# Output weights split on ScalarE and VectorE, router steps of a tile set between the matmuls of the next, ranking in two parts

## The chip, the core and the metric

The kernel runs as one program on one core of one Trainium2 chip. The metric is device time in microseconds (us) from launch to the end of the program. A core has five engines that work side by side and wait for each other through semaphores: TensorE (PE; its weight loads are listed as PEld), VectorE (DVE), ScalarE (ACT), GpSimd (POOL) and SyncE (SP), which here only issues transfers. Transfers run on 16 DMA engines of the core.

## The reference, cut to what matters

Two layers of a hybrid encoder over 528 tokens (16 learned ones, called meta, and 512 real ones) of 1024 channels. In each layer three head groups (RWKV-7, differential attention, gated linear attention) give 1024 mixed channels, an output projection adds them to the residual, and 16 experts each take their best 66 tokens:

```python
mix = jnp.concatenate([y_a, y_b, y_c], axis=-1).astype(h.dtype)
h = h + jnp.einsum("blc,cd->bld", mix, w_out[l])
h = h + expert_choice_ffn(rms_norm(h, norm2_g[l]), router[l], e_w1[l], e_w3[l], e_w2[l])

def expert_choice_ffn(u, router, w1, w3, w2):
    cap = EC_FACTOR * L // N_EXPERTS                    # 66
    aff = jax.nn.softmax(jnp.einsum("bld,de->ble", u, router).astype(jnp.float32), axis=-1)
    gates, idx = lax.top_k(jnp.swapaxes(aff, 1, 2), cap)
    xs = jax.vmap(lambda ub, ib: ub[ib])(u, idx)
    hid = jax.nn.silu(jnp.einsum("becd,edf->becf", xs, w1)) * jnp.einsum("becd,edf->becf", xs, w3)
    ys = jnp.einsum("becf,efd->becd", hid, w2) * gates[..., None].astype(u.dtype)
```

## The kernel before

Products run as three matmuls on operands that are split into a high part and a low rest: a weight `w` becomes `wh` (a copy in a shorter format) and `wl = w - wh`.

One layer goes through these stages. The input projection and the three head groups come first; the attention sweeps its 528 queries in the tiles 1, 2, 0, 3, 4 of `TOK` (tile 0 holds the 16 meta tokens, the others 128 tokens each). Its softmax is a chain of short VectorE and ScalarE steps around matmuls. While it runs, GpSimd splits the eight blocks of the output weights, `wo_h` by a copy (L966) and `wo_l` by a subtraction (L967), from two buffers `wo`.

The projection loop then takes the tiles 1, 2, 3, 4, 0. For a tile it makes two halves `c` of 512 output channels with 24 matmuls each (L1026), adds them to the residual `h` (L1029), and does the router's part: transposes `ut` (L1033) and their copies `hT`, the sum of squares (L1044) and a chain of some ten VectorE steps for the reciprocal root (L183 to L191), the logits `plg` (L1049), a softmax over 16 experts (L1052 to L1056), the transpose `pt` of it (L1058) into the table `aff` of 16 experts by tokens, and the normalised row `u`, scaled on ScalarE (L1060) and multiplied by the gain on GpSimd (L1061), which is written to `ubuf` in memory (L1062).

The ranking `top` takes the eight largest values of each expert's row at a time (L1007), finds their places (L1010) and strikes them out (L1009), nine times over 512 tokens; the 16 meta tokens are ranked apart and merged. The indices `idx` (L1078) then drive the gather of an expert's rows (L1118), an indirect transfer issued by GpSimd.

The expert stage streams 192 weight tiles of 1408 KB through nine buffers, five of which can be filled during the projection. Each half of a tile is split by ScalarE (`wh`, L1111) and VectorE (`wl`, L1112) into four buffers each, and feeds TensorE (`up_tile` and `down`, L1156 and L1217). The first four subtractions are ordered behind `idx`.

The code is written in program order, and a scheduler lays each engine's instructions out in a fixed queue of its own; within a queue they run in order. `behind(inst, mark)` keeps two instructions in that order without a wait.

Of the kernel before, what the change touches and what calls it, by code (L numbers as in the profile page):

```python
# [23 lines left out]
D = 1024  # L24
# [81 lines left out]
def body(ctx: ExitStack, tc: tile.TileContext, a, out, dbg=None, depth=DEPTH, stop=None):  # L106
# [61 lines left out]
    def behind(inst, mark):  # L168
        if mark is not None:
            tc.add_manual_dep(inst.ins, mark.ins.name,  # L170
                              mybir.DependencyInfo(mybir.DependencyClass.NoSync, mybir.DependencyReason.DATA),
                              reason="issue order")
        return inst
# [37 lines left out]
    for l in range(depth):  # L211
# [751 lines left out]
        for k in range(KT):  # L963
            w = op.tile([128, D], F32, name="wo", bufs=2)
            nc.sync.dma_start(w, a["w_out"][l, k])
            G.tensor_copy(wo_h[:, k], w)  # L966
            G.tensor_sub(wo_l[:, k], w, wo_h[:, k].bitcast(F32))  # L967
        if "a" in order:
            bank_pool("s")
            attention(ap_, *hd)  # L970
            bank_pool("mm")
        parts.close()
# [21 lines left out]
        with tc.tile_pool(name="rt", bufs=1, side="right", reuse_waits="tile") as rtp:  # L994
            g2b = rtp.tile([128, D], F32, name="g2b")
            nc.sync.dma_start(g2b, a["norm2_g"][l:l + 1].to_broadcast([128, D]))
            aff = rtp.tile([NE, SEQ], F32, name="aff")
            affm = rtp.tile([NE, NM], F32, name="affm")

            def top(x, n, name):  # L1000
                v = rtp.tile([NE, n], F32, name=f"top_v{name}")
                iu = rtp.tile([NE, n], U32, name=f"top_u{name}")
                fi = rtp.tile([NE, n], F32, name=f"top_i{name}")
# [14 lines left out]
            for t in (1, 2, 3, 4, 0):  # L1018
                o, R = TOK[t]
                p = mm_tile("po")  # L1020
                h = load_h(op, h_src, t, 3)[:R]
                for c in range(2):
                    n = 0
                    for ww, mm in ((wo_h, mh), (wo_h, ml), (wo_l, mh)):
                        for k in range(KT):
                            T.matmul(p[:R, c, :], mm[:, k, o:o + R], ww[:, k, c * 512:(c + 1) * 512],  # L1026
                                     start=(n == 0), stop=(n == 23))
                            n += 1
                    V.tensor_add(two(h)[:, c], p[:R, c], two(h)[:, c])  # L1029
                nc.sync.dma_start(hbuf[o:o + R, :], h)  # L1030
                pt = [rw_tile(q, "ut") for q in range(2)]
                for k in range(KT):
                    T.transpose(pt[k // 4][:, (k % 4) * 128:(k % 4) * 128 + R], h[:, k * 128:(k + 1) * 128],  # L1033
                                ident[:R, :R])
                hT = rtp.tile([128, 2, 4, 128], F32, name="hT", bufs=2)
                for q in range(2):
# [3 lines left out]
                    else:  # L1040
                        V.tensor_copy(hT[:, q, :, :R], src)
                u = rtp.tile([128, D], F32, name="u2", bufs=2)
# [5 lines left out]
                for k in range(KT):  # L1048
                    T.matmul(p[:R, :NE], hT[:, k // 4, k % 4, :R], rt[:, k, :], start=(k == 0), stop=(k == KT - 1))  # L1049
# [6 lines left out]
                V.tensor_scalar(lg[:R], lg[:R], mx[:R, 3:4], None, op0=OP.mult)  # L1056
                pt = sm_tile("pt")
                T.transpose(pt[:NE, :R], lg[:R], ident[:R, :R])  # L1058
                V.tensor_copy(aff[:, o - NM:o - NM + R] if t else affm, pt[:NE, :R])
                A.activation(u[:R], h, AF.Identity, scale=rs)  # L1060
                G.tensor_mul(u[:R], u[:R], g2b[:R])  # L1061
                G.dma_start(ubuf[o:o + R, :], u[:R])  # L1062
            vm, im = top(affm, NM, "m")
            va, ia = top(aff, 72, "a")
            V.tensor_scalar(ia, ia, float(NM), None, op0=OP.add)
            at_ = slice(CAP - NM, CAP)
            rev = lambda x: x[:, ::-1]
            take = rtp.tile([NE, NM], F32, name="take")
            V.tensor_tensor(take, rev(vm), va[:, at_], op=OP.is_ge)
            V.tensor_tensor(va[:, at_], va[:, at_], rev(vm), op=OP.max)  # L1070
            V.tensor_sub(im, im, rev(ia[:, at_]))
            V.tensor_mul(im, im, rev(take))
            V.tensor_add(ia[:, at_], ia[:, at_], rev(im))
# [17 lines left out]
        with tc.tile_pool(name="mw", bufs=1, reuse_waits="tile") as mw, \  # L1091
                tc.tile_pool(name="mh", bufs=1, reuse_waits="tile") as mhl, \
                tc.tile_pool(name="moe", bufs=2, reuse_waits="tile") as mo:
            ring, gathers, splits = [0], [], []
# [253 lines left out]
```

## Time and profile before

| what | us |
|---|---|
| three timed runs, median (lowest to highest) | 2734.44 (2730.94 to 2737.09) |
| the profiled execution: its own time | 2737.51 |
| the profiled execution: its span | 2735.7 |
| busy in the span: TensorE, VectorE, ScalarE, GpSimd | 2518.9, 2170.6, 1604.4, 441.3 |

The span runs from the first to the last instruction; the 1.8 us beside it lie around the program. Busy times overlap, so that they don't add up. The mean granted clock of TensorE was 0.947 of full speed. All times of the trace below are counted from the start of the span. The first layer takes about the first half of it, the second the rest.

### The profile page before, as it was taken

Reading aid. Unit: us, or ns where it says so; the run is one execution under the profiler, and the core shown is the slowest. Engines: PE = TensorE matmul, PEld = TensorE weight load, DVE = VectorE, ACT = ScalarE, POOL = GpSimd, SP = SyncE. Lnnn points to the kernel's source line nnn. Section 1 sums busy time; section 2 is a strip of 40 time slices with the busy share of each in tenths; the row PEclk is TensorE's granted clock in tenths of the full one; section 3 lists DMA queues with packets and bytes.
Section 4 is the critical chain, followed back from the end, with each engine's and each line's share of the span. In section 5 each row is a group of like instructions: output and inputs, shape, how many; then the busy total and the mean of one; then the engine's idle time right before and its main releaser. Section 6 shows DMA issues by size and latency. Waiting matters only on the chain.

```text
span 2735.7 us, 46610 instructions
## 1 busy us (share of the span) xinstructions
PE 2518.9 (92%) x18586; PEld 1981.8 (72%) x18586; DVE 2170.6 (79%) x3293; ACT 1604.4 (59%) x2107; POOL 441.3 (16%) x545
## 2 busy tenths in 40 slices
PE   7899999786999999999788899998689999999995
PEld 6778786565777777778587787755467787877783
DVE  3557667758999999999735676687589999999995
ACT  3324334425888888788542343344268888888884
POOL 3113322213000000000121133241120000000000
PEclk9878999997999999999997789999889999999998
DMA  3101101148999999999420111022499999999993
GB/s 129 47 24 60 37 25 51 64 172 312 408 400 405 403 399 409 397 412 404 174 77 32 40 44 49 13 73 93 148 358 393 413 397 411 399 409 401 407 402 117
DMA packets 84682, 643.30 MB, mean 235 GB/s; under 512 B 12592, under 2 KB 13040, under 8 KB 35312
## 3 DMA queue, kind: packets, MB, share of 16 engines
q1 hardware_dynamic: 75936, 618.16, 57.0%
q0 software_dynamic: 8528, 22.15, 3.3%
q8 instruction: 146, 2.39, 0.4%
q14 instruction: 72, 0.59, 0.1%
HBM read 617.05 MB, written 19.40 MB: 233 GB/s over the span
## 4 chain that ended last, share of the span: by engine, by line
PE 41%; DVE 5%; issue 2%; ACT 2%; DMA 1%; POOL 0%; DVEq 0%; SPq 0%; ACTq 0%; POOLq 0%
PE py L1217 9%; PE pj L288 5%; PE h1a L1156 4%; PE h3a L1156 3%; PE h1b L1156 3%; PE h3b L1156 3%; PE h1T L1156 1%; PE h3T L1156 1%; PE po L1026 1%; PE po L730 1%; DMA hbuf<-yo,idx 1%; PE S L898 1%; PE pl L473 1%; PE up L307 1%; PE py L563 0%
## 5 line engine op out<-in xcount | busy, mean ns | idle before, releaser
L1112 DVE TENSOR_TENSOR wl<-w,wh 128x1408 fp32r<-128x1408 f32 (+2 forms) x768 | 1212.7, 1617 | 59.9 <-ACT wh L1111 35.3
L1111 ACT ACTIVATE wh<-w 128x1408 fp32r<-128x1408 f32 (+2 forms) x768 | 1042.7, 1378 | 196.9 <-PE py L1217 78.5
L1217 PE MATMUL py<-wh,hh 128*66 128x512 f32 (+1 forms) x768 | 289.2, 377 | 4.3 <-ACT hh L1197 4.3
L1217 PE MATMUL py<-wh,hl 128*66 128x512 f32 (+1 forms) x768 | 288.7, 376 | 0.8 <-DVE hl L1198 0.8
L1217 PE MATMUL py<-wl,hh 128*66 128x512 f32 (+1 forms) x768 | 288.4, 375 | 0.0
L1222 POOL DMA_INDIRECT hbuf<-yo,idx x32 | 54.9, 1714 | 1190.0 <-ACT yo L1221 1076.6
L1156 PE MATMUL h1a<-wh,xx 128*66 128x512 f32 x512 | 186.1, 414 | 1.1 <-DVE xx L1134 1.1
L1156 PE MATMUL h3a<-wh,xx 128*66 128x512 f32 x512 | 182.8, 408 | 0.0
L1156 PE MATMUL h1b<-wh,xx 128*66 128x512 f32 x512 | 176.3, 410 | 0.0
L1156 PE MATMUL h3b<-wh,xx 128*66 128x512 f32 x512 | 174.7, 407 | 0.0
L1156 PE MATMUL h1T<-xx,wh 128*128 128x132 f32 x768 | 172.1, 224 | 0.0
L1156 PE MATMUL h3T<-xx,wh 128*128 128x132 f32 x768 | 171.3, 223 | 0.0
L288 PE MATMUL pj<-uh,wh 128*128 128x264 f32 (+1 forms) x896 | 166.5, 314 | 5.2 <-ACT kS L344 5.0
L288 PE MATMUL pj<-ul,wh 128*128 128x264 f32 (+1 forms) x896 | 162.2, 313 | 0.0
L288 PE MATMUL pj<-uh,wl 128*128 128x264 f32 (+1 forms) x896 | 155.6, 303 | 0.0
L1217 PEld LDWEIGHTS py<-wh,hh 128*66 128x66 f32 x768 | 105.2, 137 | 64.1 <-ACT hh L1197 4.5
L1217 PEld LDWEIGHTS py<-wl,hh 128*66 128x66 f32 x768 | 105.1, 137 | 60.6 <-issue 1.0
L1156 PE MATMUL h1T<-xx,wl 128*128 128x66 f32 x768 | 148.9, 194 | 0.0
L1156 PEld LDWEIGHTS h3T<-xx,wh 128*128 128x128 f32 x768 | 146.6, 191 | 2.7
L1156 PEld LDWEIGHTS h1T<-xx,wh 128*128 128x128 f32 x768 | 148.3, 193 | 0.0
L1156 PE MATMUL h3T<-xx,wl 128*128 128x66 f32 x768 | 148.3, 193 | 0.0
L1217 PEld LDWEIGHTS py<-wh,hl 128*66 128x66 f32 x768 | 105.3, 137 | 59.1 <-DVE hl L1198 1.5
(444 smaller groups left out, 5061.9 us busy)
## 6 DMA issues: line engine op xcount, KB each, us to landing
w<-in_e_w SPq DMA_DIRECT2D x384, 1408.0 KB, 10.9
w<-in_w_in SPq DMA_DIRECT2D x56, 512.0 KB, 3.5
wo<-in_w_out SPq DMA_DIRECT2D x16, 512.0 KB, 3.5
h<-hbuf SPq DMA_DIRECT2D x12, 512.0 KB, 4.7
swp<-raw SPq DMA_DIRECT2D x64, 66.0 KB, 2.0
h<-in_x SPq DMA_DIRECT2D x8, 512.0 KB, 7.2
hbuf<-h SPq DMA_DIRECT2D x8, 512.0 KB, 2.8
ubuf<-u POOLq DMA_DIRECT2D x8, 512.0 KB, 4.6
```

Source lines behind the costliest of these rows:

```text
L288: T.matmul(p[:M, c, :HL], ww[:, k, :M], uu[:, k, c * HL:(c + 1) * HL], start=(n == 0), stop=(n == 23))
L307: T.matmul(p[:, c, :HL], lhsT, rhs[:, c * HL:(c + 1) * HL], start=True, stop=True)
L473: T.matmul(pl[:, b, :], flat(BC[m][:, jm[m]]), az[:, m].rearrange("p x q n -> p (x q n)"), start=True, stop=True)
L730: T.matmul(o_, qd[d][hc(h), j * CH:(j + 1) * CH], kv[hc(h), d, j, :], start=False, stop=(d == 1), tile_position=(32 * h, 64 * (h % 2)))
L898: behind(T.matmul(p[:R], qk[0, h][:, qo:qo + R], qk[1, h][:, c, NM:], start=True, stop=True), mark)
L1026: T.matmul(p[:R, c, :], mm[:, k, o:o + R], ww[:, k, c * 512:(c + 1) * 512], start=(n == 0), stop=(n == 23))
L1111: A.activation(wh, w[:, lo:hi], AF.Copy)
L1112: splits.append(behind(V.tensor_sub(wl, w[:, lo:hi], wh.bitcast(F32)), chosen if len(splits) < 4 else None))
L1156: T.matmul(o_, l_, r_, start=s0, stop=s1)
L1217: T.matmul(py[:CAP, c, d0:d0 + n], x[:, kk, :], ww[:, at0 - lo:at0 - lo + n], start=(kk == 0 and i_ == 0), stop=(kk == FK - 1 and i_ == 2))
L1222: G.indirect_dma_start(out=hbuf[:, :], out_offset=bass.IndirectOffsetOnAxis(ap=idx[:CAP, e:e + 1], axis=0), in_=yo[:CAP], in_offset=None, ...
```

## The change

Four things are edited.

The output weights are no longer split by GpSimd. Four of the eight blocks are loaded ahead of the attention, and the code that splits them, copies on ScalarE and subtractions on VectorE, is written behind it.

The projection goes through the tiles 1, 2, 0, 3, 4 and runs block by block of the weights. The router's part of a tile is cut into `turn`, `affinity` and `ranked`, which are set at fixed places between the matmuls of the next tile: behind its first half, behind 12 matmuls of its second half, and behind that half. The product for `u` is one VectorE instruction.

The ranking is done in two parts: the 272 tokens of tiles 0, 1 and 2 as soon as those are through, the 256 of tiles 3 and 4 at the end, and the two lists of 66 are merged by a comparison of one with the reverse of the other.

The first four subtractions of the expert stage wait, by a semaphore, for the first gather.

```diff
+
+    def after(inst, mark):
+        tc.add_manual_dep(inst.ins, mark.ins.name,
+                          mybir.DependencyInfo(mybir.DependencyClass.Sync, mybir.DependencyReason.DATA),
+                          reason="the port is the gather's first")
...
         wo_h = op.tile([128, KT, D], F32R, name="wo_h")
         wo_l = op.tile([128, KT, D], F32R, name="wo_l")
-        for k in range(KT):
-            w = op.tile([128, D], F32, name="wo", bufs=2)
-            nc.sync.dma_start(w, a["w_out"][l, k])
-            G.tensor_copy(wo_h[:, k], w)
-            G.tensor_sub(wo_l[:, k], w, wo_h[:, k].bitcast(F32))
+        wos = ExitStack()
+        wsp = wos.enter_context(tc.tile_pool(name="wos", bufs=1, side="left", reuse_waits="tile"))
+        wo_r = []
+
+        def wo_load():
+            w = wsp.tile([128, D], F32, name="wo", bufs=4)
+            nc.sync.dma_start(w, a["w_out"][l, len(wo_r)])
+            wo_r.append(w)
+
+        for k in range(4):
+            wo_load()
         if "a" in order:
             bank_pool("s")
             attention(ap_, *hd)
             bank_pool("mm")
+        for k in range(KT):
+            A.activation(wo_h[:, k], wo_r[k], AF.Copy)
+            V.tensor_sub(wo_l[:, k], wo_r[k], wo_h[:, k].bitcast(F32))
+            if len(wo_r) < KT:
+                wo_load()
+        wos.close()
...
-            aff = rtp.tile([NE, SEQ], F32, name="aff")
-            affm = rtp.tile([NE, NM], F32, name="affm")
+            early = TOK[3][0]
+            aff = rtp.tile([NE, L], F32, name="aff")
...
-                fi = rtp.tile([NE, n], F32, name=f"top_i{name}")
+                fi = iu.bitcast(F32)
...
-            for t in (1, 2, 3, 4, 0):
+            def turn(t, h):
                 o, R = TOK[t]
-                p = mm_tile("po")
-                h = load_h(op, h_src, t, 3)[:R]
-                for c in range(2):
-                    n = 0
-                    for ww, mm in ((wo_h, mh), (wo_h, ml), (wo_l, mh)):
-                        for k in range(KT):
-                            T.matmul(p[:R, c, :], mm[:, k, o:o + R], ww[:, k, c * 512:(c + 1) * 512],
-                                     start=(n == 0), stop=(n == 23))
-                            n += 1
-                    V.tensor_add(two(h)[:, c], p[:R, c], two(h)[:, c])
                 nc.sync.dma_start(hbuf[o:o + R, :], h)
                 pt = [rw_tile(q, "ut") for q in range(2)]
                 for k in range(KT):
-                    T.transpose(pt[k // 4][:, (k % 4) * 128:(k % 4) * 128 + R], h[:, k * 128:(k + 1) * 128],
-                                ident[:R, :R])
+                    mark = T.transpose(pt[k // 4][:, (k % 4) * 128:(k % 4) * 128 + R], h[:, k * 128:(k + 1) * 128],
+                                       ident[:R, :R])
...
+                return hT, mark
+
+            def affinity(t, h, p, hT):
+                o, R = TOK[t]
...
+                    mark = T.matmul(p[:R, :NE], hT[:, k // 4, k % 4, :R], rt[:, k, :], start=(k == 0),
+                                    stop=(k == KT - 1))
...
+                return lg, u, rs, mark
+
+            def ranked(t, h, lg, u, rs):
+                o, R = TOK[t]
                 pt = sm_tile("pt")
                 T.transpose(pt[:NE, :R], lg[:R], ident[:R, :R])
-                V.tensor_copy(aff[:, o - NM:o - NM + R] if t else affm, pt[:NE, :R])
-                A.activation(u[:R], h, AF.Identity, scale=rs)
-                G.tensor_mul(u[:R], u[:R], g2b[:R])
+                V.tensor_copy(aff[:, o:o + R], pt[:NE, :R])
+                V.scalar_tensor_tensor(u[:R], h, rs, g2b[:R], op0=OP.mult, op1=OP.mult)
                 G.dma_start(ubuf[o:o + R, :], u[:R])
-            vm, im = top(affm, NM, "m")
-            va, ia = top(aff, 72, "a")
-            V.tensor_scalar(ia, ia, float(NM), None, op0=OP.add)
-            at_ = slice(CAP - NM, CAP)
-            rev = lambda x: x[:, ::-1]
-            take = rtp.tile([NE, NM], F32, name="take")
-            V.tensor_tensor(take, rev(vm), va[:, at_], op=OP.is_ge)
-            V.tensor_tensor(va[:, at_], va[:, at_], rev(vm), op=OP.max)
-            V.tensor_sub(im, im, rev(ia[:, at_]))
-            V.tensor_mul(im, im, rev(take))
-            V.tensor_add(ia[:, at_], ia[:, at_], rev(im))
+
+            tops, last = {}, None
+            for t in (1, 2, 0, 3, 4):
+                o, R = TOK[t]
+                p = mm_tile("po")
...
+
+                def project(terms, mark=None):
+                    for k, i, c in terms:
+                        ww, mm = ((wo_h, mh), (wo_h, ml), (wo_l, mh))[i]
+                        behind(T.matmul(p[:R, c, :], mm[:, k, o:o + R], ww[:, k, c * 512:(c + 1) * 512],
+                                        start=(k == 0 and i == 0), stop=(k == KT - 1 and i == 2)), mark)
+                        mark = None
+
+                ki = [(k, i) for k in range(KT) for i in range(3)]
+                if last is None:
+                    project([(k, i, c) for k, i in ki for c in range(2)])
+                else:
+                    project([(k, i, 0) for k, i in ki])
+                    hT, mark = turn(*last[:2])
+                    project([(k, i, 1) for k, i in ki[:12]], mark)
+                    lg, u, rs, mark = affinity(*last, hT)
+                    project([(k, i, 1) for k, i in ki[12:]], mark)
+                    ranked(*last[:2], lg, u, rs)
+                    if last[0] == 0:
+                        tops["a"] = top(aff[:, :early], 72, "a")
+                for c in range(2):
+                    V.tensor_add(two(h)[:, c], p[:R, c], two(h)[:, c])
+                last = t, h, p
+            hT, mark = turn(*last[:2])
+            lg, u, rs, mark = affinity(*last, hT)
+            ranked(*last[:2], lg, u, rs)
+            va, ia = tops["a"]
+            vb, ib = top(aff[:, early:], 72, "b")
+            V.tensor_scalar(ib, ib, float(early), None, op0=OP.add)
+            rev = lambda x: x[:, CAP - 1::-1]
+            take = rtp.tile([NE, CAP], F32, name="take")
+            V.tensor_tensor(take, rev(vb), va[:, :CAP], op=OP.is_gt)
...
                 A.activation(wh, w[:, lo:hi], AF.Copy)
-                splits.append(behind(V.tensor_sub(wl, w[:, lo:hi], wh.bitcast(F32)),
-                                     chosen if len(splits) < 4 else None))
+                sub = V.tensor_sub(wl, w[:, lo:hi], wh.bitcast(F32))
+                if len(splits) < 4:
+                    after(sub, first[0])
+                splits.append(sub)
...
+                    first.append(gather)
```

Where the scheduler puts the splits is seen in the queues. VectorE in the attention of layer 0, at the end of tile 1's normalisation (the reciprocal root of the attention's output, `o`), before:

```order
L190 SCALAR_TENSOR_TENSOR rq_u<-rq_u,rq_w 128x4
L892 TENSOR_REDUCE mxm<-smeta 128x8
L191 SCALAR_TENSOR_TENSOR rq_y<-rq_u,rq_y 128x4
L810 SCALAR_TENSOR_TENSOR rq_y<-rq_y,st 128x4
L813 TENSOR_TENSOR o<-o,rq_y 128x512
L840 TENSOR_REDUCE st<-S 128x1
```

and with the change:

```order
L196 SCALAR_TENSOR_TENSOR rq_u<-rq_u,rq_w 128x4
L986 TENSOR_TENSOR wo_l<-wo,wo_h 128x1024
L197 SCALAR_TENSOR_TENSOR rq_y<-rq_u,rq_y 128x4
L898 TENSOR_REDUCE mxm<-smeta 128x8
L816 SCALAR_TENSOR_TENSOR rq_y<-rq_y,st 128x4
L986 TENSOR_TENSOR wo_l<-wo,wo_h 128x1024
L819 TENSOR_TENSOR o<-o,rq_y 128x512
L926 COPY wt<-pt 128x512
```

The subtractions stand inside the attention's queue, the first two here, the other six within the next 22 rows. The corresponding copies on ScalarE stand likewise inside the attention. GpSimd's queue, which held the eight pairs, before:

```order
L592 TENSOR_TENSOR Y<-Y,pw 128x128 x2
L966 CAST wo_h<-wo 128x1024
L967 TENSOR_TENSOR wo_l<-wo,wo_h 128x1024
L966 CAST wo_h<-wo 128x1024
L967 TENSOR_TENSOR wo_l<-wo,wo_h 128x1024
L866 MEMSET st 128x16
L966 CAST wo_h<-wo 128x1024
L967 TENSOR_TENSOR wo_l<-wo,wo_h 128x1024
```

with the change it holds neither these nor the multiplications of L1061.

TensorE in the projection, from the end of one tile to the middle of the next, before:

```order
L1026 MATMUL po<-wo_l,mxh 128x512 x8
L1058 MATMUL pt<-cst,lg 16x128
L1026 MATMUL po<-wo_h,mxh 128x512 x12
L1026 MATMUL po<-wo_h,mxl 128x512 x8
L1026 MATMUL po<-wo_l,mxh 128x512 x8
L1033 MATMUL ut<-cst,h 128x128 x4
L1026 MATMUL po<-wo_h,mxh 128x512 x2
L1033 MATMUL ut<-cst,h 128x128 x4
L1049 MATMUL plg<-rt,hT 128x16 x4
L1026 MATMUL po<-wo_h,mxh 128x512 x2
```

and with the change at tile 0, whose second half begins behind the transposes of tile 2:

```order
L1089 MATMUL po<-wo_h,mxl 16x512
L1089 MATMUL po<-wo_l,mxh 16x512
L1041 MATMUL ut<-cst,h 128x128 x8
L1089 MATMUL po<-wo_h,mxh 16x512
L1089 MATMUL po<-wo_h,mxl 16x512
L1089 MATMUL po<-wo_l,mxh 16x512
```

Before, the transposes and logits of a tile directly followed its last matmuls, and the next tile stopped at them; now they stand half a tile later. The logits follow 12 matmuls behind these rows, and the transpose `pt` ends the tile.

VectorE at the end of the projection, with the change: the last rows of the ranking of 272 tokens and the additions of tile 4 (L1106), then the router chain of tiles 3 and 4:

```order
L195 TENSOR_SCALAR rq_w<-rq_u 128x1
L1028 MAX_INDEX top_ua<-top_va,aff 16x8
L196 SCALAR_TENSOR_TENSOR rq_u<-rq_u,rq_w 128x1
L1106 TENSOR_TENSOR h<-po,h 128x512
L1030 CAST top_ua<-top_ua 16x72
L197 SCALAR_TENSOR_TENSOR rq_y<-rq_u,rq_y 128x1
L1106 TENSOR_TENSOR h<-po,h 128x512
L1066 TENSOR_SCALAR mx<-mx,rq_y 128x1
L1077 SCALAR_TENSOR_TENSOR u_6682<-h,rq_y,g2b 128x1024
L1068 RECIPROCAL mx<-mx 128x1
```

The additions of tile 4 stand behind the whole first ranking. Behind the second ranking, from the indices to the expert stage, VectorE's queue was

```order
L1077 COPY gates<-pt 66x16
L1078 CAST idx<-pt 66x16
L1112 TENSOR_TENSOR wl<-w,wh 128x1408 x4
L1134 TENSOR_TENSOR xx<-ptx,xx 128x4x66 x2
L1112 TENSOR_TENSOR wl<-w,wh 128x1408 x7
```

and is now

```order
L1124 COPY gates<-pt 66x16
L1125 CAST idx<-pt 66x16
L1159 TENSOR_TENSOR wl<-w,wh 128x1408
L1184 TENSOR_TENSOR xx<-ptx,xx 128x4x66 x2
L1159 TENSOR_TENSOR wl<-w,wh 128x1408 x10
```

One subtraction, which waits for the gather, stands ahead of the preparation of the gathered rows (`xx`), and the other three behind it.

## Rows read from the trace of the kernel before

**Rows 1.** Engine busy time in stretches of layer 0; granted clock, DMA share, GB/s.

```profile
core 0: us, PE busy (x) PEld busy (x) DVE busy (x) ACT busy (x) POOL busy (x), PEclk, DMA share, GB/s
468.00:500.00 32.00, 19.62 (x121) 12.21 (x119) 28.59 (x52) 6.83 (x21) 27.83 (x17) 0.92 0.47 172
500.00:530.00 30.00, 27.02 (x125) 15.31 (x125) 25.74 (x98) 21.16 (x73) 0.07 (x1) 0.86 0.08 29
547.00:612.00 65.00, 57.46 (x307) 41.83 (x305) 31.45 (x89) 13.11 (x26) 11.73 (x8) 1.00 0.48 167
612.00:640.00 28.00, 2.75 (x23) 2.07 (x23) 21.40 (x68) 8.11 (x11) 11.74 (x6) 0.54 0.59 197
800.00:900.00 100.00, 100.00 (x645) 78.69 (x644) 97.09 (x86) 80.73 (x76) 5.92 (x4) 1.00 1.01 400
```

**Rows 2.** Waits in the first expert stage, 640 to 1330: total, times, longest.

```profile
ACT wh L1111 <- PE py L1217: 32.5, 61, 0.7
...
PE h1a L1156 <- DVE xx L1134: 0.6, 1, 0.6
```

**Rows 3.** Timeline, two rows of the attention: start, duration, engine, instruction.

```profile
490.19 2.35 POOL L967 TENSOR_TENSOR wo_l<-wo,wo_h 128x1024 fp32r<-128x1024 f32 x1
...
490.37 2.19 DVE L183 TENSOR_SCALAR rq_y<-ms 128x4 int32<-128x4 int32 x1
```

**Rows 4.** VectorE groups, 468 to 500.6: first and last of twelve lengthened.

```profile
L909 DVE SCALAR_TENSOR_TENSOR e<-e,st 128x512 f32<-128x512 f32 x2 | 3.6, 1801 | 0.0
...
L853 DVE TENSOR_SCALAR mq<-cst,st 128x64 f32<-128x64 f32 x1 | 0.8, 782 | 0.0
```

**Rows 5.** VectorE groups, 500.6 to 545.2: the same kinds later.

```profile
L909 DVE SCALAR_TENSOR_TENSOR e<-e,st 128x512 f32<-128x512 f32 x8 | 6.0, 744 | 0.0
...
L807 DVE TENSOR_SCALAR ms<-ms 128x4 f32<-128x4 f32 x2 | 0.3, 166 | 0.0
```

**Rows 6.** The page's costliest groups: VectorE subtraction of an expert half.

```profile
L1112 DVE TENSOR_TENSOR wl<-w,wh 128x1408 fp32r<-128x1408 f32 (+2 forms) x768 | 1212.7, 1617 | 59.9 <-ACT wh L1111 35.3
```

**Rows 7.** Timeline of one projection tile, 556 to 573, TensorE and VectorE.

```profile
556.62 0.28 PE L1058 MATMUL pt<-cst,lg 128*16 128x128 f32 x1 [1.66 <-DVE lg L1056]
...
564.18 0.66 PE L1033 MATMUL ut<-cst,h 128*128 128x128 f32 x4
...
564.67 0.96 PE L1049 MATMUL plg<-rt,hT 128*128 128x16 f32 x8
...
570.46 1.88 DVE L1056 TENSOR_SCALAR lg<-lg,mx 128x16 f32<-128x16 f32 x1
...
572.39 0.28 PE L1058 MATMUL pt<-cst,lg 128*16 128x128 f32 x1 [1.59 <-DVE lg L1056]
```

**Rows 8.** Timeline from the last projection to the first expert matmul.

```profile
604.75 0.68 DVE L1007 MAX8 top_va<-aff 16x8 f32<-16x512 f32 x1
...
606.80 0.66 DVE L1007 MAX8 top_va<-top_xa 16x8 f32<-16x512 f32 x1
...
608.28 2.02 PE L1026 MATMUL po<-wo_l,mxh 128*16 128x512 f32 x8
...
625.12 0.19 DVE L1065 TENSOR_SCALAR top_ia<-top_ia 16x72 f32<-16x72 f32 x1
...
626.67 0.16 DVE L1078 CAST idx<-pt 66x16 int32<-66x16 f32 x1
...
626.75 6.22 DVE L1112 TENSOR_TENSOR wl<-w,wh 128x1408 fp32r<-128x1408 f32 x4
...
627.75 6.10 POOL L1118 DMA_INDIRECT xg<-ubuf,idx  x1 [4.38 <-DVE idx L1078]
...
634.16 0.95 POOL L1118 DMA_INDIRECT xg<-ubuf,idx  x1 [0.30 <-issue]
...
639.39 0.69 PE L1156 MATMUL h1a<-wh,xx 128*66 128x512 f32 x1 [0.56 <-DVE xx L1134]
```

**Rows 9.** Timeline, GpSimd, the first gather of layer 1.

```profile
1983.16 6.14 POOL L1118 DMA_INDIRECT xg<-ubuf,idx  x1 [4.35 <-DVE idx L1078]
```

More of the change, by code (lines that the diff above doesn't have):

```diff
@@ L172, in behind @@
                               reason="issue order")
+        return inst
+    def after(inst, mark):
+        tc.add_manual_dep(inst.ins, mark.ins.name,
+                          mybir.DependencyInfo(mybir.DependencyClass.Sync, mybir.DependencyReason.DATA),
+                          reason="the port is the gather's first")
         return inst
@@ L1048, in body @@
                 for k in range(KT):
-                    T.matmul(p[:R, :NE], hT[:, k // 4, k % 4, :R], rt[:, k, :], start=(k == 0), stop=(k == KT - 1))
+                    mark = T.matmul(p[:R, :NE], hT[:, k // 4, k % 4, :R], rt[:, k, :], start=(k == 0),
+                                    stop=(k == KT - 1))
                 lg = rtp.tile([128, NE], F32, name="lg", bufs=2)
@@ L1072, in body @@
-            V.tensor_mul(im, im, rev(take))
-            V.tensor_add(ia[:, at_], ia[:, at_], rev(im))
+            tops, last = {}, None
+            for t in (1, 2, 0, 3, 4):
+                o, R = TOK[t]
+                p = mm_tile("po")
+                h = load_h(op, h_src, t, 3)[:R]
+                def project(terms, mark=None):
[19 more added lines that the diff above has]
+                last = t, h, p
@@ new lines, in body @@
+            hT, mark = turn(*last[:2])
[7 more added lines that the diff above has]
+            V.tensor_tensor(take, rev(vb), va[:, :CAP], op=OP.is_gt)
+            V.tensor_tensor(va[:, :CAP], va[:, :CAP], rev(vb), op=OP.max)
@@ L1074, in body @@
+            V.tensor_sub(ib[:, :CAP], ib[:, :CAP], rev(ia))
+            V.tensor_mul(ib[:, :CAP], ib[:, :CAP], rev(take))
+            V.tensor_add(ia[:, :CAP], ia[:, :CAP], rev(ib))
             pt = sm_tile("pt")
@@ L1093, in body @@
                 tc.tile_pool(name="moe", bufs=2, reuse_waits="tile") as mo:
-            ring, gathers, splits = [0], [], []
+            ring, gathers, splits, first = [0], [], [], []
             def wtile(src):
```

## The prediction

> **What bounds the kernel now.** I read the stages of layer 0 first, as a table of busy time by stretch. In the expert stage TensorE is busy for 100 us of 100, VectorE for 97 [rows 1]; the list of waits has ScalarE waiting there for TensorE to free its buffers, and TensorE for VectorE once, for 0.6 us [rows 2]. So TensorE sets the pace, the weight transfers keep up, and what is won ahead of the stage is won at the end, provided the stage keeps its pace. The three stretches ahead of it are not bound by TensorE. In the attention from 468 to 500 VectorE is busy for 28.6 us of 32, yet with only 52 instructions, against 98 in the next 30 us, while GpSimd is busy for 27.8. From 547 to 612, the projection, TensorE is busy for 57.5 of 65. From 612 to 640 it does almost nothing (2.8 of 28) [rows 1]: router, ranking and gather stand on the path there. The timeline of these stretches was read next, and the change touches all three.
>
> **The attention.** The timeline shows a VectorE instruction on 128x4 elements that lasts 2.19 us, from just behind the start of GpSimd's subtraction to its end [rows 3]; the same kinds take 0.17 and 0.74 us later [rows 5]. Between 468 and 500.6 twelve kinds are lengthened so, with one or two instructions each, from 1.8 us for one of L909 down to 0.8 for L853 [rows 4]. Mean less usual duration, summed over the twelve, is 17.3 us. A check from the stretches: at the later rate of 25.74 us for 98 instructions, 52 would take 13.7, so that 14.9 were lost [rows 1]. I take 17.3, since these instructions are named one by one.
>
> With the change GpSimd reads nothing there, and this goes. VectorE gets eight subtractions of 1024 columns instead. From 0.744 us for 512 [rows 5] and 1.617 for 1408 [rows 6], one of 1024 costs 1.24, eight 9.9. ScalarE's eight copies fall into its idle time: it was busy for 6.8 us of 32 [rows 1]; without that cover some 8 us would stand ahead of the exponentials. VectorE gains 17.3 - 9.9 = 7.4 us. The pause also left TensorE at a granted clock of 0.92 and then 0.86 of full speed, so at 1.2 in place of 2.4 GHz for part of the time [rows 1]; I add 1 us for this. Gain: **8.4 us** a layer. From below: four buffers hold half the blocks, the later four are loaded behind the subtractions that free them, and VectorE's queue waits with attention work behind it; 4 us remain if half is lost so. From above: 11, if the lower clock goes altogether.
>
> **The projection.** A tile takes 15.8 us: from one transpose `pt` to the next, 556.62 to 572.39 [rows 7]. At the end of it TensorE has issued all it may, and idles for 1.6 us until VectorE has finished the softmax; its last step on 128x16 elements takes 1.88 us [rows 7], lengthened by GpSimd's product for `u` as in the attention. With this step goes a shorter stop of the weight loads; I count 2.1 us of waiting per tile. Now the router's steps of a tile have the whole next tile of time. The logits cost TensorE up to 0.96 us in each of two halves [rows 7], as before, and each of the short steps should be done when its place comes: the sum of `h` is some 5 us old at the transposes; the logits end at about 11 us into the tile of 13.7, and the softmax needs 1.2 more. So 15.8 becomes 13.7. Four tiles follow tile 1: 4 x 2.1 = 8.4. One of them now carries the router of the 16 meta tokens in place of a full one, which goes to the tail: 1.2. Some 0.2 comes from two fewer matmuls behind the attention. Gain: **9.8 us** a layer. From below 5, if the softmax misses its place; from above 10.5, all idle time and the lighter router.
>
> **The tail.** Before, the last projection matmul ends at 610.3 and the first of the experts starts at 639.4, 29.1 us later [rows 8]. Now, counted from the last projection matmul:
> - The sums of tile 4 lie behind the first ranking on VectorE. A round of the ranking takes 2.05 us over 512 tokens (604.75 to 606.80) [rows 8], in three passes over them. From 0.744 us for 512 elements [rows 5] and 1.617 for 1408 [rows 6] an element more costs 0.97 ns; three passes over 240 fewer save 0.70, so 1.35 a round over 272 and 1.30 over 256, and for nine rounds, the last without the striking out, 11.6 and 11.2. The first ranking starts, by my estimate, 1.2 us into tile 4, and ten root steps of tile 3 (0.17 each, as in [rows 5]) and one sum (some 0.7) go between: sums done 15.2 us after the tile's start, 1.5 behind its last matmul.
> - From the second transposes of a tile to its `pt` it took 8.2 us (564.18 to 572.39), 1.7 of it by the lengthened L1056 [rows 7]. Now two products for `u` stand on VectorE in that chain, some 1.2 each like the subtractions of 1024 columns: 8.9, to 10.4.
> - The second ranking: 11.2, to 21.6. Merge, two transposes and `idx`: 1.7 (625.12 to 626.83), to 23.3; 0.9 to the gather's start (626.83 to 627.75) [rows 8]: 24.2.
> - The gather. Before, it occupied GpSimd for 6.10 us, and the next, with VectorE at rest, for 0.95. Four subtractions ran from 626.75 for 6.22 us, to 632.97, and the gather ended 0.88 later, at 633.85 [rows 8]; layer 1 repeats it with 6.14 [rows 9]. So it waits for them, and alone takes 0.95: to 25.1.
> - From its end to the first expert matmul 5.5 us passed (633.85 to 639.39) [rows 8]: the landing of the rows and their preparation. One subtraction (1.6) now runs ahead of the latter, most of it within the landing; I add 0.5. First expert matmul at **31.1**, 2.0 us later than before.
>
> The other three subtractions are behind that; TensorE starts at half clock as before (0.54 in 612 to 640 [rows 1]), and VectorE, at 1.6 us a half [rows 6], is ahead of it again before it is needed. I cost this at nothing; its cover is that slow start. Bounds of the tail: 4 us longer, when the chain of tile 4 meets a busy VectorE at each step, to 1 us shorter.
>
> The Trainium skill bears on one step of this. The page SBUF — State Buffer, section Who interferes with whom, says that a `tensor_tensor` takes only the read side of the port pair that VectorE and GpSimd share, while writing a gather's descriptors needs the write side, so that such a subtraction would not hold the gather up (it calls this inferred). The two ends 0.88 us apart speak against it; by the rule the 6.1 us would stay, and the first rival below is what then happens.
>
> **Sum.** Per layer 8.4 + 9.8 - 2.0 = 16.2 us, for both 32.4. The profiled execution took 2737.51 us, 1.8 of it around the span; less 32.4 it is 2705.1. It lay 3.1 above the median of the runs shown, so the prediction for the median is 2734.4 - 32.4 = **2702 us**.
>
> **Rivals.**
> 1. *The gather stays slow.* If its 6.1 us are its own (a first gather behind new indices), the wait only puts the subtractions behind it. For: both first gathers take 6.1. Against: both end 0.88 us behind the subtractions. The tail grows by 5.2 a layer: 2712. Chance 0.10.
> 2. *The attention gains nothing.* VectorE's queue stops at the subtractions for weights or for ScalarE. For: VectorE is busy for 25.7 of 30 us without the disturbance [rows 1], and takes 9.9 us more. Against: the sum above. With a gain of 1 the layer wins 8.8: 2717. Chance 0.10.
> 3. *The fixed places come too early.* The softmax leaves a little over 1 us of room. If TensorE waits 1.2 us in each of four tiles, the layer wins 11.4: 2712. Chance 0.10.
> 4. *The expert stage loses its pace* (the other side). VectorE enters it three halves behind, has 3 us of room in 100 [rows 1], and never fills its buffers, so that its bursts between experts reach TensorE. From 1.0 us an expert on, over 32 experts, this eats the 32 us; at 1.4 it costs 45: 2747. Against: a half takes TensorE at the lower clock twice as long as VectorE's subtraction, which refills the buffers within the first two. Chance 0.05.
> 5. *All bounds fall well*: attention 11, projection 10.5, tail no longer than before: 43 in all, 2691. Chance 0.06.
>
> The change as such cannot be without effect, since the queues of three engines differ; that its gains and losses cancel within 0.2% (5.5 us, about what a measurement of this kernel can tell from no change) has 0.04.
>
> **How the numbers follow.** The sum as worked out, within some 7 us (2695 to 2709), has 0.55. With rivals 1, 2, 3 and 5 the kernel is faster by over 0.2% with 0.91; I give 0.90, 0.04 to no change and 0.06 to slower. The range of 8 in 10 takes in the sum and the rivals 1 to 3, and at its lower end almost all of 5: 2690 to 2717.
>
> **What the next profile would show.** Right: no VectorE instruction on a few elements above 1 us between 468 and 500, and the next query tile's maxima (L899 now) some 8 us earlier; tiles 13.7 us apart in the projection, with TensorE busy throughout; the first gather at about 1 us on GpSimd; 31 us from the last projection matmul to the first of the experts; the expert stage as long as before. The prediction is wrong if VectorE stands idle ahead of the new subtractions, if TensorE idles at the transposes, logits or `pt`, if the gather keeps its 6 us, or if TensorE waits for `wl` in the expert stage.

## Result and profile after

The changed kernel took 2700.61 us (median of four runs, 2698.94 to 2704.05); the kernel before took 2733.12 beside it. The ratio is 0.9881, with a 95% interval of 0.9864 to 0.9898: faster by 32.5 us, where 32.4 had been forecast.

The profiled execution took 2698.94 us, 38.6 less than that of before. To see where they went, both layers were cut at five landmarks of TensorE: *ahead* ends with the start of the last gate matmul `pg` of the RWKV heads, *attention* with that of the last transposes `pf` of the attention's norm, *projection* with the end of the last projection matmul, *tail* with the first expert matmul, *experts* with the end of the last matmul `py`. The table is worked out from the timelines (us; the two layers of each kernel):

```
kernel                                      ahead           attention      projection     tail           experts
before                                      457.0 / 458.5   86.0 / 85.9    67.3 / 67.3    29.1 / 29.6    714.7 / 714.2
after                                       456.2 / 456.4   76.7 / 75.5    58.5 / 58.5    30.7 / 30.7    714.1 / 713.8
e1 split on GpSimd again                    457.0 / 459.0   83.5 / 83.8    58.7 / 58.7    31.8 / 31.2    714.4 / 713.1
e2 without the wait for the gather          460.3 / 458.2   75.5 / 76.8    58.5 / 58.5    36.0 / 35.3    714.5 / 713.6
e3 one ranking of 528                       458.6 / 455.6   76.7 / 75.5    58.5 / 58.5    34.6 / 34.4    713.7 / 713.9
e4 subtractions behind mq                   458.3 / 455.8   78.4 / 76.5    59.9 / 59.9    29.7 / 29.9    713.2 / 714.7
e5 subtractions spread                      455.7 / 459.9   75.9 / 75.9    52.5 / 52.5    30.1 / 31.1    714.7 / 713.1
e6 idle matmuls in the tail                 455.2 / 459.9   75.4 / 75.8    58.5 / 58.5    30.6 / 31.8    713.6 / 713.1
e7 product for u on GpSimd again            453.2 / 460.3   75.1 / 75.6    58.5 / 58.5    34.9 / 34.4    714.8 / 713.7
e8 as e5, first ranking late                454.9 / 455.3   75.9 / 75.9    52.5 / 52.5    29.5 / 28.8    714.2 / 714.7
e9 before, the split alone                  459.9 / 456.5   76.9 / 76.0    68.9 / 68.9    28.6 / 28.7    714.5 / 714.7
e10 before, the wait alone                  456.3 / 455.9   84.3 / 86.5    67.3 / 68.9    25.0 / 23.7    713.1 / 713.3
```

On the mean of the layers the attention is 9.8 us shorter, the projection 8.8, and the tail 1.3 longer: 17.3 a layer, 34.6 for both. Of the other 4 us of the profiled pair 1.1 lie in the experts and 2.9 ahead of the attention. There only the first four weight loads of the change stand (from 420.8 us on), and the kernels scatter between 453 and 460 us whatever was edited, so no cause is given for these 2.9.

Busy time in stretches of the kernel after, to be read beside [rows 1] (it runs some 19 us ahead by the end of the projection, hence other bounds):

```profile
468.00:500.00 32.00, 26.30 (x137) 15.49 (x133) 25.89 (x75) 18.09 (x41) 0.11 (x1) 0.89 0.25 86
500.00:530.00 30.00, 28.98 (x162) 20.82 (x161) 24.76 (x99) 19.73 (x67) 0.00 (x0) 1.00 0.14 49
547.00:591.00 44.00, 44.00 (x239) 31.77 (x238) 24.91 (x99) 6.23 (x15) 1.07 (x2) 1.00 0.43 164
591.00:622.00 31.00, 6.51 (x38) 4.92 (x36) 21.22 (x81) 8.28 (x13) 4.54 (x6) 0.58 0.51 173
800.00:900.00 100.00, 100.00 (x617) 76.13 (x616) 97.34 (x86) 80.81 (x75) 5.94 (x4) 1.00 1.01 406
```

Between 468 and 500 VectorE now has 75 instructions in place of 52 in less busy time, and GpSimd almost none. From 547 to 591 TensorE is busy for 44 us of 44. The tail still has little of it, at a granted clock of 0.58, and the expert stage reads as before.

VectorE groups of the kernel after, 468 to 491 (mean ns of one behind the comma), against [rows 3 to 5]:

```profile
L986 DVE TENSOR_TENSOR wo_l<-wo,wo_h 128x1024 fp32r<-128x1024 f32 x8 | 9.7, 1219 | 1.0 <-ACT wo_h L985 1.0
...
L915 DVE SCALAR_TENSOR_TENSOR e<-e,st 128x512 f32<-128x512 f32 x2 | 1.5, 746 | 0.0
...
L189 DVE TENSOR_SCALAR rq_y<-ms 128x4 int32<-128x4 int32 x2 | 0.3, 167 | 0.0
```

A step on 128x4 elements takes 0.17 us again, the product on 128x512 takes 0.75, and the eight subtractions took 1.22 each, where 1.24 had been estimated. What they cost beside their own time shows on TensorE (timeline; in brackets the idle time ahead and what ended it). Before, its longest stop there was for the norm `o` of tile 2:

```profile
500.68 1.12 PE L816 MATMUL pf<-cst,o 128*128 128x128 f32 x4 [9.29 <-DVE o L813]
```

After:

```profile
486.63 1.97 PE L865 MATMUL pt<-mq,me 128*128 128x64 f32 x8 [3.11 <-DVE mq L862]
...
489.08 4.92 PE L877 MATMUL po<-vB,mq 128*16 128x128 f32 x24 [0.47 <-ACT mq L871]
...
490.78 1.28 DVE L905 TENSOR_REDUCE st<-S 128x1 f32<-128x512 f32 x2
...
493.93 0.66 PE L822 MATMUL pf<-cst,o 128*128 128x128 f32 x4
```

The 9.3 us for `o` are gone. In their place TensorE waits 3.11 us for `mq`, a product on 64 columns, in whose chain four of the subtractions stand on VectorE (480.54 to 486.30), and the clock falls, to 0.50 of full speed from 488 to 492: the batch of 24 small matmuls takes 4.92 us. Before, it stood at 0.50 from 496 to 506, behind the longer stop. The next maxima (L905) come at 490.78, 9.8 us earlier than before, 0.9 of it from ahead of the attention; some 8 had been expected.

The projection of the kernel after, transposes `pt` and one last softmax step, against [rows 7]:

```profile
550.57 0.27 PE L1075 MATMUL pt<-cst,lg 128*16 128x128 f32 x1
...
562.93 0.23 DVE L1069 TENSOR_SCALAR lg<-lg,mx 128x16 f32<-128x16 f32 x1
...
564.37 0.27 PE L1075 MATMUL pt<-cst,lg 128*16 128x128 f32 x1
...
577.19 0.18 PE L1075 MATMUL pt<-cst,lg 16*16 16x16 f32 x1
```

The step that took 1.88 us takes 0.23, none of these `pt` waits, and they stand 13.8 and (with the router of the 16 meta tokens) 12.8 us apart.

Its tail, against [rows 8]:

```profile
590.97 0.40 PE L1089 MATMUL po<-wo_l,mxh 128*128 128x512 f32 x1
...
592.18 0.67 DVE L1106 TENSOR_TENSOR h<-po,h 128x512 f32<-128x512 f32 x1
...
595.05 0.28 PE L1075 MATMUL pt<-cst,lg 128*16 128x128 f32 x1 [1.42 <-DVE lg L1069]
...
595.16 2.78 PE L1061 MATMUL plg<-rt,hT 128*128 128x16 f32 x16
...
599.55 1.27 DVE L1077 SCALAR_TENSOR_TENSOR u<-h,rq_y,g2b 128x1024 f32<-128x1024 f32 x1
...
601.22 0.38 PE L1075 MATMUL pt<-cst,lg 128*16 128x128 f32 x1 [3.28 <-DVE lg L1069]
...
601.95 0.42 DVE L1025 MAX8 top_vb<-aff 16x8 f32<-16x256 f32 x1
...
603.21 0.40 DVE L1025 MAX8 top_vb<-top_xb 16x8 f32<-16x256 f32 x1
...
614.44 0.16 DVE L1125 CAST idx<-pt 66x16 int32<-66x16 f32 x1
...
615.52 1.00 POOL L1167 DMA_INDIRECT xg<-ubuf,idx  x1 [13.87 <-DVE idx L1125]
...
620.05 1.62 DVE L1159 TENSOR_TENSOR wl<-w,wh 128x1408 fp32r<-128x1408 f32 x1 [5.45 <-issue]
...
622.08 0.69 PE L1206 MATMUL h1a<-wh,xx 128*66 128x512 f32 x1 [0.91 <-DVE xx L1184]
```

The gather takes 1.00 us in place of 6.10, and the subtractions come behind the landing of its rows. The first of the two `pt` is that of tile 3. By the code it ends tile 4; it comes 3.7 us behind the last matmul (591.37), and waits.

### The profile page after: what moved, and what is told of

It reads as the page before. It is cut to its first block, busy times and chain, and to the rows that moved or that the text cites. A ratio compares the mean times of both kernels' runs of the same rounds, so it can differ in the third digit from the quotient of the medians.

```text
span 2697.2 us, 46680 instructions
## 1 busy us (share of the span) xinstructions
PE 2513.8 (93%) x18586; PEld 1983.7 (74%) x18586; DVE 2158.7 (80%) x3389; ACT 1608.8 (60%) x2113; POOL 351.8 (13%) x503
```

## The experiments

Each run was timed in five rounds beside the kernel before, whose medians were 2733.06 us (e1 to e4), 2733.59 (e5 to e7) and 2735.67 (e8 to e10). The stages are those of the table.

**e1, the split undone.**

```diff
-            A.activation(wo_h[:, k], wo_r[k], AF.Copy)
-            V.tensor_sub(wo_l[:, k], wo_r[k], wo_h[:, k].bitcast(F32))
+            G.tensor_copy(wo_h[:, k], w)
+            G.tensor_sub(wo_l[:, k], w, wo_h[:, k].bitcast(F32))
```

> The changed kernel with the output weights split on GpSimd ahead of the attention again (two buffers), all else as changed. My theory (the attention wins about 10 us a layer, because GpSimd no longer blocks VectorE): some 10 us a layer are given back, 2720 us, and VectorE steps of 1 to 2 us on a few elements stand beside GpSimd's subtractions again. Rival (the win has to do with the new order of the tiles and of the blocks, the split is hidden anyway): under 2 us a layer, at most 2704.

Measured: 2718.85 us, ratio 0.9941 (0.9925 to 0.9958). The attention is 7.5 us longer than in the kernel after, the projection stays. Timeline of TensorE:

```profile
498.83 1.12 PE L822 MATMUL pf<-cst,o 128*128 128x128 f32 x4 [7.34 <-DVE o L819]
```

TensorE waits for the norm `o` as in the kernel before, for 7.3 us. The mechanism holds. The size is 2.3 us short of the 9.8 that the change won. VectorE's queue in layer 0 is the same in both kernels with the split on GpSimd, up to `o`; which of its instructions GpSimd's meet is not. The kernel before, and below it e1 (timeline):

```profile
497.73 2.34 POOL L967 TENSOR_TENSOR wo_l<-wo,wo_h 128x1024 fp32r<-128x1024 f32 x1
...
497.90 2.72 DVE L813 TENSOR_TENSOR o<-o,rq_y 128x512 f32<-128x512 f32 x1
```

```profile
498.09 0.69 DVE L819 TENSOR_TENSOR o<-o,rq_y 128x512 f32<-128x512 f32 x1
...
498.11 2.87 POOL L973 TENSOR_TENSOR wo_l<-wo,wo_h 128x1024 fp32r<-128x1024 f32 x1
```

Behind the start of GpSimd's last subtraction `o` took 2.72 us, just ahead of it 0.69, as much as the stops of 9.3 and 7.3 differ by.

**e9, the split alone** in the kernel before (the same edit the other way round).

> The kernel before with only the split of the output weights changed (loads in four buffers, copies on ScalarE and subtractions on VectorE, written behind the attention). My theory (the parts add up): the attention is 7.5 to 10 us shorter in each layer, projection and tail as before: 2713 to 2718. Rival (part of the win of the attention belongs to the projection's new order of blocks, which TensorE interleaves with it): 4 to 6 us a layer, 2721 to 2725.

Measured: 2720.47 us, ratio 0.9937 (0.9922 to 0.9952). The attention is as short as in the kernel after (9.5 us won), the tail is 0.7 shorter, but the projection took 1.6 us more in both layers. Stretches of its last two projection tiles, layer 0:

```profile
584.00:596.00 12.00, 12.00 (x66) 8.11 (x64) 3.51 (x16) 3.13 (x6) 0.58 (x1) 1.00 0.17 69
596.00:600.00 4.00, 1.94 (x7) 0.72 (x7) 3.93 (x6) 0.00 (x0) 2.34 (x2) 0.85 0.21 83
600.00:605.00 5.00, 5.00 (x19) 1.86 (x18) 4.76 (x13) 0.00 (x0) 0.00 (x0) 0.78 0.12 43
```

Where the last tile waits for the softmax the granted clock went down to 0.85 and 0.78. In the profile of before the same place kept 1.00 in both layers; in e10 the matmuls slowed in layer 1 and not in layer 0, by the same 1.5 us. So the time of 2720 missed the expected 2713 to 2718, the attention's share did not, and the rival, that TensorE's interleaving belongs to it, falls.

**e2, the wait undone.**

```diff
-                    after(sub, first[0])
+                    behind(sub, chosen)
```

> The changed kernel with the first four subtractions of the expert stage ordered behind the indices, as before, without the wait for the first gather. My theory (the gather cannot finish while VectorE subtracts without a pause): the first gather takes about 6.1 us, ends 0.9 behind the fourth subtraction, and the first expert matmul starts 5 us later in each layer: 2710 us. Rival (such a subtraction does not hold the gather up; its time of before came from elsewhere): the gather keeps 1.0 us, the rows land as now, and the four subtractions end at about that time: 2700 to 2702.

Measured: 2712.75 us (2706 to 2723), ratio 0.9920 (0.9900 to 0.9940). Timeline:

```profile
617.87 6.22 DVE L1159 TENSOR_TENSOR wl<-w,wh 128x1408 fp32r<-128x1408 f32 x4
...
618.87 6.10 POOL L1167 DMA_INDIRECT xg<-ubuf,idx  x1 [13.86 <-DVE idx L1125]
...
630.22 0.69 PE L1206 MATMUL h1a<-wh,xx 128*66 128x512 f32 x1 [0.56 <-DVE xx L1184]
```

The gather starts 1.0 us behind the first subtraction, takes 6.10 us and ends 0.9 behind the fourth. The first expert matmul comes 5 us later in both layers.

**e10, the wait alone** in the kernel before.

> The kernel before with only the wait of the first four subtractions of the expert stage for the first gather. My theory (the subtractions hold the gather up, whatever lies ahead): the gather takes 1.0 us, and the first expert matmul starts some 4.5 us earlier in each layer: 2724. Rival (in the tail of before the loads or the landing end last): within 1 us a layer, 2731 to 2734.

Measured: 2727.31 us, ratio 0.9965 (0.9952 to 0.9978). The gather takes 1.02 us, and the tail 24.3 in place of 29.4: 5.0 a layer. The median shows 8.4 of these 10 (the profiled execution is the fastest of eight, 2722 to 2732).

**e3, one ranking.**

```diff
-                    if last[0] == 0:
-                        tops["a"] = top(aff[:, :early], 72, "a")
...
-            va, ia = tops["a"]
-            vb, ib = top(aff[:, early:], 72, "b")
...
+            va, ia = top(aff, 72, "a")
```

> The changed kernel with one ranking over all 528 tokens at the end, in place of 272 and 256 with a merge. My theory (rounds cost by tokens: 2.1 us a round over 528, about 1.2 over 256): ranking 7.5 us longer, the merge of 1 us saved, and the router chain of tiles 3 and 4 up to 2 earlier, as VectorE has no first ranking to do beside it: 4.5 to 6.5 us a layer, 2710 to 2713. Rival (the first ranking costs what it saves, since it stands on VectorE ahead of the last tile's sums): no change, 2700.

Measured: 2707.97 us, ratio 0.9899 (0.9885 to 0.9914). The tail is 3.8 us longer, a little under the 4.5 expected. The ranking in two parts is worth that, not more: the first part takes VectorE from the router steps of tiles 3 and 4. Without it `pt` of tile 3 stands at its place, and that of tile 4 comes 7.6 us behind the projection in both layers, where it came 9.9 and 10.3 with the change.

**e7, the product for `u` on ScalarE and GpSimd again.**

```diff
-                V.scalar_tensor_tensor(u[:R], h, rs, g2b[:R], op0=OP.mult, op1=OP.mult)
+                A.activation(u[:R], h, AF.Identity, scale=rs)
+                G.tensor_mul(u[:R], u[:R], g2b[:R])
```

> The changed kernel with the product for u on ScalarE and GpSimd again, as before. My theory (a tile of the projection now has time to hide a lengthened softmax step; the fixed places win, not the move of u): the tiles stay 13.8 us apart, and only the tail changes, by the GpSimd products of tiles 3 and 4 against two VectorE products of 1.27 us: within 1.5 us a layer, 2698 to 2704. Rival (GpSimd's product was what made the tiles 15.8 us long): 1 to 2 us a tile come back, 2708 to 2714.

Measured: 2706.79 us, ratio 0.9899 (0.9884 to 0.9914). Timeline of its tail, VectorE and GpSimd:

```profile
589.00 2.34 POOL L1078 TENSOR_TENSOR u<-u,g2b 128x1024 f32<-128x1024 f32 x1 [19.98 <-ACT u L1077]
...
589.89 1.48 DVE L1069 TENSOR_SCALAR lg<-lg,mx 128x16 f32<-128x16 f32 x1
...
598.36 2.34 POOL L1078 TENSOR_TENSOR u<-u,g2b 128x1024 f32<-128x1024 f32 x1 [6.13 <-ACT u L1077]
...
598.85 1.89 DVE L1069 TENSOR_SCALAR lg<-lg,mx 128x16 f32<-128x16 f32 x1
```

The projection keeps its 58.5 us with GpSimd's product in it, so the fixed places alone won there. But the tail is 4 us longer, where 1.5 at most had been expected: there the last softmax step stands in the chain, and ends with GpSimd's product again. The two steps shown are together 2.9 us longer than with the change (0.23 each); the cause of the last 1 us is open.

**e4, the subtractions behind `mq`.**

```diff
-            V.tensor_sub(wo_l[:, k], wo_r[k], wo_h[:, k].bitcast(F32))
+            behind(V.tensor_sub(wo_l[:, k], wo_r[k], wo_h[:, k].bitcast(F32)), mqs[-1])
```

> The changed kernel with the eight subtractions for the output weights ordered behind the weights mq of the meta queries on VectorE, of which TensorE now waits 3.1 us. My theory (the subtractions stand ahead of a step that TensorE waits for, and VectorE idles 3 us later): TensorE's wait goes, and with the clock that it loses there 2 to 5 us a layer are won: 2690 to 2696. Rival (VectorE is the bound of the attention as a whole, so that the order does not matter): 2700. The other side (the next tile's maxima now wait behind the subtractions): 2703 to 2706.

Measured: 2704.67 us, ratio 0.9899 (0.9882 to 0.9916). That is within the other side's range, but the interval overlaps that of the change; the attention is 1.3 us longer than with the change and the projection 1.4. Nothing was won. Timeline of TensorE:

```profile
482.27 1.00 PE L865 MATMUL pt<-mq,me 128*128 128x64 f32 x8
...
495.96 1.12 PE L822 MATMUL pf<-cst,o 128*128 128x128 f32 x4 [8.19 <-DVE o L819]
```

`mq` is no longer waited for, and the stop moved to the next step behind the subtractions, the norm `o` of tile 2: 8.19 us in place of 3.11.

**e5, the subtractions spread.** Blocks 2 to 7 are ordered behind the norms of the tiles 2, 0 and 3, two each.

```diff
-            V.tensor_sub(wo_l[:, k], wo_r[k], wo_h[:, k].bitcast(F32))
+            behind(V.tensor_sub(wo_l[:, k], wo_r[k], wo_h[:, k].bitcast(F32)), normed[k // 2] if k > 1 else None)
```

> The changed kernel with six of the eight subtractions for the output weights ordered late on VectorE: two behind the norm (o) of tile 2, two behind that of tile 0, two behind that of tile 3, so that neither the meta weights mq nor the norm of tile 2 stand behind them. My theory (what is left of the stall of the attention is the order on VectorE, which idles 3 us behind it): TensorE's waits for mq and o go, 2 to 4 us a layer, 2692 to 2697. Rival (VectorE's work, not its order, bounds the attention): within 1 us a layer, 2698 to 2702. The other side: the weights come too late for the first projection tile, whose matmuls then wait: 2703 to 2710.

Measured: 2690.58 us, ratio 0.9846 (0.9833 to 0.9860), some 10 us below the change and a little below the time expected. Timeline of TensorE, and below it the projection's matmuls alone in one stretch:

```profile
482.18 1.00 PE L865 MATMUL pt<-mq,me 128*128 128x64 f32 x8
...
483.65 3.23 PE L877 MATMUL po<-vB,mq 128*16 128x128 f32 x28 [0.47 <-ACT mq L871]
...
486.86 0.66 PE L822 MATMUL pf<-cst,o 128*128 128x128 f32 x4
```

```profile
500.00:532.00 32.00, 15.84 (x60) 10.70 (x60) 1.00 0.13 40
```

Neither step is waited for, 28 of the small matmuls take 3.23 us, where 24 had taken 4.92, and `pf` of tile 2 comes 7 us earlier. By the last `pf` only 1.3 of that is left in layer 0 and nothing in layer 1, since the six subtractions stand ahead of it now. TensorE used the difference: up to 532 it ran 60 of the first tile's matmuls, against this in the kernel after:

```profile
500.00:532.00 32.00, 8.49 (x32) 5.96 (x33) 1.00 0.13 46
```

So the projection takes 6 us less in each layer. VectorE's work is the same as with the change, so these 6 us were lost by its order.

**e8, e5 with the first ranking written behind the router steps of tile 4.**

```diff
-                    if last[0] == 0:
-                        tops["a"] = top(aff[:, :early], 72, "a")
...
-            va, ia = tops["a"]
+            va, ia = top(aff[:, :early], 72, "a")
```

> The kernel of the run e5_spread with the first ranking (272 tokens) written behind the router steps of tile 4, so that on VectorE its rounds fill what these leave free, in place of standing ahead of them. My theory (the tail is bound by VectorE's queue, where the chain of tile 4 waits 2.3 us for its logits while the rest of tile 3's steps lie ahead): the transposes pt of tile 4 come 2 us earlier and the tail is 2 us shorter in each layer, 2686 to 2688. Rival (the tail is one chain of sums, logits at half clock, softmax and second ranking, which the first ranking does not touch): 2690 to 2691.

Measured: 2687.62 us, ratio 0.9823 (0.9806 to 0.9840). The tail is 0.6 us shorter than in e5 in layer 0 and 2.3 in layer 1, where 2 in each had been expected. Timeline of TensorE, layer 0:

```profile
583.13 0.27 PE L1075 MATMUL pt<-cst,lg 128*16 128x128 f32 x1
...
591.90 0.38 PE L1075 MATMUL pt<-cst,lg 128*16 128x128 f32 x1 [3.96 <-DVE lg L1069]
```

`pt` of tile 3 is at its place, ahead of the end of the last projection matmul (583.29), so the first ranking had held it up. `pt` of tile 4 comes 8.6 us behind that end, 9.2 in e5. In layer 1 1.4 of the 2.3 us are the logits of tile 4, which took 3.44 us in e5 and 2.04 here. This is the fastest version found; the interval of its ratio overlaps that of e5.

**e6, idle matmuls in the tail**, whose results nothing uses.

```diff
+            def warm(n, mark):
+                p = rw_tile(0, "warm")
+                for _ in range(n):
+                    mark = behind(T.matmul(p[:, :128], ident, ident, start=True, stop=True), mark)
+                return mark
```

> The changed kernel with idle matmuls (128x128 of the identity, result unused) on TensorE in the tail: 40 behind the last pt, 20 behind the transposes of the indices. It tells what the half clock at the start of the expert stage costs, and whether the three subtractions behind the gather are covered by it alone. Theory of the prediction (the slow start is the cover of VectorE): the clock is at full speed at the first expert matmul, but TensorE then waits for wl, and at most 1 us a layer is won: 2698 to 2701. Rival (VectorE is ahead in any case): the 4.4 us at half clock are halved, some 2 us a layer, 2696; if the idle matmuls outlast the ranking or the gather, their excess stands on the path and the time goes up by it.

Measured: 2697.07 us, ratio 0.9861 (0.9846 to 0.9876), which can't be told from the change. Two of the four executions took 2693, the others 2701, and the trace is of one of the latter; what the two faster ones did is not known. Timeline of TensorE and two stretches:

```profile
611.85 4.73 PE L1084 MATMUL warm<-cst 128*128 128x128 f32 x40
...
617.59 0.71 PE L1186 MATMUL ptx<-cst,xg 66*128 66x66 f32 x8 [1.01 <-DMA xg<-ubuf,idx]
...
619.65 0.45 PE L1213 MATMUL h1a<-wh,xx 128*66 128x512 f32 x1 [1.34 <-DVE xx L1191]
```

```profile
616.00:620.00 4.00, 1.65 (x17) 1.27 (x16) 2.38 (x4) 0.67 (x2) 2.06 (x2) 1.00 0.83 199
620.00:624.00 4.00, 4.00 (x21) 3.31 (x19) 4.00 (x3) 1.38 (x1) 0.06 (x1) 0.62 1.02 371
```

The idle matmuls end ahead of the gather, and the first expert matmul runs at full clock (0.45 us). But between them TensorE had waited for the rows and for `xx`, and from 620.8 the clock is down again. So in the traced execution the half clock was mostly not taken away, and neither theory is tested.

## Why the prediction was right, point by point

**The attention, 8.4 us forecast, 9.8 measured.** The lengthened steps went, as e1 and e9 show from both sides (rival 2 is out), and a subtraction lasted 1.22 us, about as worked out. Mis-sized was VectorE's term, 17.3 - 9.9 = 7.4 us. From the start of the attention to the next maxima (457.12 to 500.55 before, 456.27 to 490.78 after) VectorE was busy for 39.6 us before and 30.9 after, 39.8 and 30.9 in layer 1: some 8.7 less, with about as much idle time. In e5, where six of the eight subtractions stand behind that point, it is 24.8. So a subtraction cost VectorE 1.0 us there, not 1.24: its neighbours overlap with it by some 0.1 us at either end. From the maxima to the last `pf` 0.4 us more were won in layer 0 and 2.0 in layer 1, where the prediction had 1 us for the clock; which part of them is the clock's, no run separates. The bound from below did not come: at the subtractions VectorE's queue waited for 1.0 us in all, but their place in it cost TensorE 3.1 us for `mq`. e5 shows that more was to be had than the upper bound of 11 a layer: it wins 6 us more, counted in the projection, by the order on VectorE.

**The projection, 9.8 forecast, 8.8 measured.** In the four tiles behind tile 1 each step but one was done when its place came, and rival 3 is out. The missing 1.0 are small terms: a tile takes 13.8 and not 13.7, that with the meta router 12.8 and not 12.5, and tile 4, to the end of its last matmul, 14.2. That the fixed places won it, and not the new order of tiles and blocks, is read from the waits that are gone and from e7; no run undoes the places alone. The step that was late is the softmax of tile 3, at the end of tile 4: there VectorE is in the first ranking (e3 and e8 show it), and its `pt` fell into the tail.

**The tail, 31.1 forecast, 30.7 measured.** From the last matmul (591.37) the steps came at: sums 1.5 (forecast 1.5), `pt` 9.9 (10.4), `idx` 23.2 (23.3), gather's start 24.2 (24.2), gather 1.00 (0.95), and 5.6 more to the first expert matmul (6.0). A round over 256 tokens took 1.26 us, in place of 1.30. The half microsecond for the subtraction ahead of `xx` was not seen. These are of layer 0; in layer 1 `pt` came at 10.3, and the tail is as long.

**The gather.** Rival 1 falls by e2 and e10: the same subtractions, without and with the wait, make it 6.1 and 1.0 us in either kernel, at 5 us a layer. The Trainium skill, page SBUF — State Buffer, section Who interferes with whom, infers that a `tensor_tensor` leaves free the side of the port that descriptors are written by, and so these subtractions would not hold the gather up. The measurement decides against that: in every run with the wait the first gather took 1.00 to 1.02 us in both layers, in every run without it 6.10 to 6.15. By which resource they hold it up, no run shows.

**The expert stage.** It did not lose its pace (714.7 and 714.2 us before, 714.1 and 713.8 after), so rival 4 is out. That the slow start covers VectorE's three late halves stays unproven: TensorE waited for no `wl` in e6 either, but its clock had not stayed up.

That the forecast gain of 32.4 us meets the measured 32.5 is partly luck. Per layer 1.4 us too little was forecast for the attention's gain, 1.0 too much for the projection's, and 0.7 too much for the tail's loss. What does not cancel, 1.1 a layer, is seen in the stages of the profiled pair (34.6) and not in the medians.

## What to carry to other kernels

Look for VectorE instructions that last far longer than their kind, and for what GpSimd does meanwhile: here GpSimd's work, moved to VectorE itself, took some 8 us of VectorE's time in a layer, and the same time fell by 8.7 all the same. Then see what stands behind the moved work in its new queue: with the same eight subtractions on VectorE, attention and projection together were 16, 19 or 25 us a layer shorter than before (e4, the change, e5), and only their places differ between the three. An order of two engines (here the subtractions behind the gather) can be worth as much as work removed, and is cheap to try alone.

## What the hardware showed beside that

The granted clock of TensorE fell after short gaps, and not always. At the end of the projection of the kernel after, behind waits of 0.8 and 1.4 us, it was 0.97 from 594 to 596 and 0.50 from 596 to 598, and the logits of tile 4 took 2.78 us, where those of tiles 1 and 2 took 1.85. One gap of 2 us in the last tile of the projection cost 1.5 us in some places (e9, e10 layer 1) and nothing in others (before, e10 layer 0). What decides between them these runs don't show.
